# A 32-expert DiT block on one core: one more area for the weight stream, a new order of the last two experts, and the rare branch moved behind the stores

## The chip, the cores and the metric

The kernel runs on one core of one Trainium2 chip. The metric is device microseconds of one execution, the median of three runs. Weights, activations and sums are all float32, apart from a few small masks.

## The reference, cut to what matters

One block of a diffusion transformer for 256 tokens of 1024 features: modulated norm, two attentions (global and windowed), a gated merge, then a mixture of 32 experts of which each token uses four, and a last norm.

```
h2 = modulate(rms_norm(x, norm2_g), sh2, sc2)
top_logit, top_idx = top_k(h2 @ w_router + b_router, 4)
for e in range(32):
    u = h2 @ w_e1[e] + b_e1[e]                       # 1024 -> 2048
    act = glu * sigmoid(1.702 * glu) * (lin + 1)     # even and odd columns of u, clipped at 7
    out = out + combine[:, e] * (act @ w_e2[e] + b_e2[e])
x = rms_norm(x + g2 * out, final_g)
```

An expert's matrices are 8.39 MB (`w_e1`) and 4.19 MB (`w_e2`), 403 MB in all.

## The kernel before, in words

**The stream.** All large weights go through one list, `pieces`, in a fixed order. `pump` (line 96) issues them on the queue of SyncE (SP) as long as there is room: a 2 MB piece of an expert takes a whole area of 16 KB a partition, smaller pieces take half of one. `N_PAIR` (line 25) areas are allotted at the start (`areas`, line 88); after the attention `grow` (line 147) adds the buffers `xx` and `ptt` (lines 636 and 637), so that the experts have nine. `done` (line 142) gives an area back when the last matmul on it has been written into the program, and calls `pump`; on the chip SP then waits at that DMA until the readers are through. The names `ring`, `xx` and `ptt` in the profile are these areas.

**The experts.** Each expert works on up to 64 gathered tokens (`CAP`, line 19). `gather` (822) brings the tokens of a pair of experts together with matmuls, `bias1` (709) starts the sums in PSUM with the bias, `gemm1` (854) multiplies with the first matrix in eight slices `k` of 1 MB, `act` (867) does the activation on VectorE (DVE) and ScalarE (ACT), `act_turn` (880) transposes the result, and `gemm2` (890) multiplies with the second matrix. The stationary operand has 64 columns, so two matmuls share the array, one in each half of its columns. `spread` (838) makes the matrix that weighs and returns a pair's tokens, and `scatter` (912) applies it and adds to the sum `ACC`. The loop at line 974 interleaves them: scatter half of the pair before, the bias and slice 0 of expert e+1, turn e, slice 1 of e+1, `gemm2` of e, slices 2 to 7 of e+1, its activation. The order of all queues is the order of the program text (`manual_schedule`).

**The last expert** (lines 986 to 1167) has a path of its own. Its first matrix comes in eight pieces `l1`, its second in four pieces `l2`, each of 1 MB in two DMAs of 512 KB that read runs of 2 KB (lines 121 to 132). `half1` works through one half of the hidden columns, `act_half` and `turn_half` follow, `gemm2` of expert 30 stands between. Expert 30 and expert 31 are not returned as a pair: `scatter_e0` (1014) starts the sums of expert 30 in four PSUM tiles, and the last matmuls (1149) add expert 31 to them. A last norm is formed from squares of `ACC` by halves of 512 columns, and four stores of 256 KB leave at line 1167.

**The branch.** If an expert has more than 64 tokens, the block under `tc.If(cnt > CAP)` (line 1041) computes the rest for all experts. It stands between the pieces `half1(1, 1)` and `half1(1, 2)`, and with this input it is skipped, but all five engines load `cnt` (line 1040) and branch around it.

**Small DMAs.** `g2`, a gate of 1024 numbers, is written to DRAM (line 670) and read back to all partitions (751); `b2` (754) and the last norm's gain `fg` (755) come likewise. All four are issued by GpSimd (POOL).

Of the kernel before, what the change touches and what calls it, by code (L numbers as in the profile page):

```python
# [24 lines left out]
N_PAIR = 7  # L25
# [9 lines left out]
def tile_dit_block(ctx: ExitStack, tc: tile.TileContext, xcT, consts, small, rows,  # L35
                   w_m0, w_q, w_mod, w_in, w_br, w_o, w_r, w1, b1, w2, b2, out):
# [21 lines left out]
    def halves1():  # L58

        pieces.extend(("l1", q, None) for q in range(8))  # L60

    def halves2():
        pieces.extend(("l2", q, None) for q in range(4))

# [31 lines left out]
    def pump():  # L96
        while n_next[0] < len(pieces):
# [23 lines left out]
            if kind == "l2":  # L121
                h, q = divmod(idx, 2)
                for b in range(2):
                    nc.sync.dma_start(
                        out=t[:, 1024 * b:1024 * b + 1024].rearrange("p (k c) -> p k c", k=2),
                        in_=w2[NE - 1, b].rearrange("p (q k c) -> p q k c", q=2, k=2)[:, q, :, 512 * h:512 * h + 512])
            elif kind == "l1":
                h, q = divmod(idx, 4)
                for b in range(2):
                    nc.sync.dma_start(  # L130
                        out=t[:, 1024 * b:1024 * b + 1024].rearrange("p (a c) -> p a c", a=2),
                        in_=w1[NE - 1, q].rearrange("p (b a h c) -> p b a h c", b=2, a=2, h=2)[:, b, :, h, :])
            elif kind == "q":
# [536 lines left out]
    nc.gpsimd.dma_start(out=g2_dram.rearrange("o (b p) -> (o b) p", b=8), in_=g2t)  # L670
# [83 lines left out]
    nc.gpsimd.dma_start(out=be2, in_=b2)  # L754
    nc.gpsimd.dma_start(out=fg, in_=rows[0:1, 1024:2048].to_broadcast([128, 1024]))
# [98 lines left out]
    def gemm1(e, u, ks, between=None):  # L854
        p, j = divmod(e, 2)
        for k in ks:
            w = take("w1", (e, k // 2))[:, 2048 * (k % 2):2048 * (k % 2) + 2048]
# [4 lines left out]
            if k % 2:  # L862
                done("w1", (e, k // 2))
            if between and k in between:
                between[k]()
# [24 lines left out]
    def gemm2(e, aT):  # L890
# [10 lines left out]
        if e >= NE - 2:  # L901
            YY[e] = x_t[:, 0, 512 * (e % 2):512 * (e % 2) + 512]
            nc.vector.tensor_tensor(out=YY[e], in0=y, in1=g2x, op=ALU.mult)
            return
# [15 lines left out]

    def scatter_one(e, tb):

        for h in range(2):
            s = slice(512 * h, 512 * h + 512)
            sp = ps2.tile([128, 512], F32, name="sp", tag=("sp", "xg")[tb], bufs=2)
            nc.tensor.matmul(sp, TT[e][64 * h:64 * h + 64, tb, :], YY[e][64 * h:64 * h + 64, :],
                             start=True, stop=True)
            nc.vector.tensor_tensor(out=ACC[0][:, tb, s], in0=ACC[0][:, tb, s], in1=sp, op=ALU.add)

    def settle():  # L930
# [10 lines left out]
        for tb in range(2):  # L941
            for h in range(2):
# [3 lines left out]
                t = per.tile([128, 512], F32, name="bt", tag="msb")  # L946
# [12 lines left out]
    def steps(e):  # L959

        p, j = divmod(e, 2)
        if e >= NE - 2:
            return {4: lambda: spread(e, (e, e))}
        if j == 0:
            return {3: lambda: spread(p, (e, e + 1)), 5: lambda: pick(p + 1)}
# [20 lines left out]
    e0, e1 = NE - 2, NE - 1  # L986
    sums = {}

    def half1(h, q, u):
        w = take("l1", 4 * h + q).rearrange("p (b a c) -> p b a c", b=2, a=2)  # L990
        for b in range(2):
            k = 2 * q + b
            for i in range(2):
                nc.tensor.matmul(u[64 * i:64 * i + 64, h, :], XT[e1 // 2][:, k, 64:128], w[:, b, i, :],  # L994
                                 start=False, stop=(k == 7))
        done("l1", 4 * h + q)

    def act_half(h, u):
        t, c = tmp4, slice(256 * h, 256 * h + 256)
        glu, sg, lin = t[:, 0, c], t[:, 1, c], t[:, 2, c]  # L1000
        nc.vector.tensor_scalar(out=glu, in0=u[:, h, 0:256], scalar1=LIMIT, scalar2=None, op0=ALU.min)  # L1001
        nc.scalar.activation(out=sg, in_=glu, func=AF.Sigmoid, scale=ALPHA)  # L1002
        nc.vector.tensor_scalar(out=lin, in0=u[:, h, 256:512], scalar1=LIMIT, scalar2=-LIMIT, op0=ALU.min,
                                op1=ALU.max)
        nc.vector.tensor_tensor(out=glu, in0=glu, in1=sg, op=ALU.mult)
        nc.vector.scalar_tensor_tensor(out=glu, in0=lin, scalar=1.0, in1=glu, op0=ALU.add, op1=ALU.mult)

    def turn_half(h):
        tp = ps2.tile([128, 4, 128], F32, name="ta", tag="tp")
        for b in range(2):  # L1010
            nc.tensor.transpose(tp[:, b, :], tmp4[:, 0, 256 * h + 128 * b:256 * h + 128 * b + 128], ident)
        nc.scalar.copy(out=tmp4[:, 3, 256 * h:256 * h + 256].rearrange("p (b s) -> p b s", b=2), in_=tp[:, 0:2, :])  # L1012

    def scatter_e0(h):
# [5 lines left out]
    scatter(NE // 2 - 2, (0,))  # L1020
    u = bias1(e1)
    half1(0, 0, u)
    aT = act_turn(e0)
    half1(0, 1, u)
    scatter(NE // 2 - 2, (1,))
    g2x = per.tile([128, 512], F32, name="g2x", tag="msb")
    for h in range(2):
        nc.vector.tensor_copy(g2x[64 * h:64 * h + 64, :], g2[64 * h:64 * h + 64, 512 * h:512 * h + 512])
    gemm2(e0, aT)
    half1(0, 2, u)  # L1030
    half1(0, 3, u)
    act_half(0, u)
    half1(1, 0, u)
    scatter_e0(0)
    turn_half(0)
    spread(e1, (e1, e1))
    half1(1, 1, u)
# [3 lines left out]
    with tc.If(cnt > CAP):  # L1041
# [20 lines left out]
        def body(e):  # L1062
# [40 lines left out]
            for tb in range(2):  # L1103
                aT = y_t[0][:, tb, :].rearrange("p (k s) -> p k s", k=8)
                for h in range(2):
# [4 lines left out]
                    t = per.tile([128, 512], F32, name="bt", tag="msb")  # L1110
# [12 lines left out]
    nc.scalar.activation(out=junk, in_=eps, func=AF.Sqrt)  # L1123
    fin = moe.tile([128, 2, 4], F32, name="fin")
    aT = tmp4[:, 3, :].rearrange("p (b s) -> p b s", b=4)
    yl = [ps2.tile([128, 512], F32, name="yl", tag="y")]

    def half2(h, q):
        w = take("l2", 2 * h + q).rearrange("p (k c) -> p k c", k=4)
        for b in range(4):  # L1130
            k = 2 * q + 4 * (b // 2) + b % 2

            nc.tensor.matmul(yl[h][64 * (k % 2):64 * (k % 2) + 64, :], aT[:, k % 4, 64 * (k // 4):64 * (k // 4) + 64],  # L1133
                             w[:, b, :], start=(q == 0 and b < 2), stop=(q == 1 and b >= 2))

    half2(0, 0)
    turn_half(1)
    yl.append(ps2.tile([128, 512], F32, name="yl", tag="tp"))
    half2(0, 1)
    half2(1, 0)  # L1140
    for h in range(2):
        s = slice(512 * h, 512 * h + 512)
        if h:
            half2(1, 1)
        yy = x_t[:, h, 512:1024]
        nc.vector.tensor_tensor(out=yy, in0=yl[h], in1=g2[:, s], op=ALU.mult)  # L1146
        for tb in range(2):
            a = ACC[0][:, tb, s]
            nc.tensor.matmul(sums[tb, h], TT[e1][:, tb, :], yy, start=False, stop=True)  # L1149
            nc.vector.tensor_tensor(out=a, in0=a, in1=sums[tb, h], op=ALU.add)  # L1150
            nc.scalar.activation(out=y_t[0][:, tb, s], in_=a, func=AF.Square, accum_out=fin[:, tb, h:h + 1])  # L1151
            if h == 0:
                nc.vector.tensor_scalar(out=fin[:, tb, 2:3], in0=fin[:, tb, 0:1], scalar1=1.0 / 1024, scalar2=EPS,  # L1153
                                        op0=ALU.mult, op1=ALU.add)
                nc.gpsimd.tensor_tensor(out=a, in0=a, in1=fg[:, s], op=ALU.mult)
            else:
                nc.scalar.activation(out=fin[:, tb, 3:4], in_=fin[:, tb, 1:2], func=AF.Sqrt, bias=fin[:, tb, 2:3],  # L1157
                                     scale=1.0 / 1024)
    for tb in range(2):
# [99 lines left out]
```

## Time and profile before

| | |
|---|---|
| runs | 1209.86, 1210.23 and 1211.34 us; median 1210.23 us |
| the profiled execution | 1209.79 us, of which the profile's span is 1208.0 us |
| mean granted TensorE clock | 0.996 |
| busy in the span | PE 1147.9, PEld 531.5, DVE 360.0, ACT 138.8, POOL 35.1 us |
| read from HBM | 456.36 MB, on average 379 GB/s over the span |

How to read it: PE is the matmul engine, PEld its weight load, which overlaps. PE's busy time is no measure of need: matmuls are pipelined, and one that stands behind others counts as busy. The figures of the DMA engines by stretch tell more. Times in rows are microseconds from the span's start unless marked ns; an arrow in brackets names what ended an engine's idle time.

### The profile page before, as it was taken

The numbers are of one execution on the slowest core, as the hardware profiler recorded it, in microseconds if no ns is written. First come the engines' busy times: TensorE is split into PE (matmuls) and PEld (weight loads), VectorE is DVE, ScalarE is ACT, GpSimd is POOL, SyncE is SP. The second block draws the span as 40 slices with busy tenths as digits, with TensorE's granted clock in tenths as the row PEclk, the third lists the DMA queues.
The fourth block names the chain that finished last, engine by engine and source line by source line (L and its number), as shares of the span: only waits on it lengthen the run. The fifth ranks groups of instructions, "written<-read, shape, count | busy, mean of one in ns | idle before, by whom it ended". The sixth has DMA issues, their size and how long they took to land. (4 is left out here: it accounts for less than half of the span.)

```text
span 1208.0 us, 13270 instructions
## 1 busy us (share of the span) xinstructions
PE 1147.9 (95%) x5624; PEld 531.5 (44%) x5624; DVE 360.0 (30%) x765; ACT 138.8 (11%) x304; POOL 35.1 (3%) x29
## 2 busy tenths in 40 slices
PE   7999999999999999999999999999999899999986
PEld 5888666883333424343434343333333232323221
DVE  3363665332122242223222221212222222222222
ACT  2122553021000000000000000000000000000002
POOL 0231100000000000000000000000000000000000
PEclk9999999999999999999999999999999999999998
DMA  9976641978999999999999999999999999999992
GB/s 379 385 301 213 240 175 53 352 296 335 427 428 428 427 427 428 427 427 428 427 429 427 428 428 425 430 427 427 429 426 426 428 428 428 429 426 429 417 396 89
DMA packets 43279, 458.32 MB, mean 379 GB/s; under 512 B 4872, under 2 KB 5264, under 8 KB 13776
## 3 DMA queue, kind: packets, MB, share of 16 engines
q1 hardware_dynamic: 41520, 454.05, 90.3%
q10 hardware_dynamic: 1296, 2.06, 0.5%
q0 software_dynamic: 400, 1.32, 0.3%
q8 instruction: 46, 0.75, 0.2%
q14 instruction: 17, 0.14, 0.0%
HBM read 456.36 MB, written 1.05 MB: 379 GB/s over the span
## 5 line engine op out<-in xcount | busy, mean ns | idle before, releaser
L860 PE MATMUL u<-ring,t 128*64 128x512 f32 x1472 | 337.3, 599 | 19.6 <-DMA ring<-w 19.2
L860 PEld LDWEIGHTS u<-ring,t 128*64 128x64 f32 x1472 | 100.7, 137 | 214.2 <-issue 178.2
L897 PE MATMUL y<-ring,r_q 128*64 128x512 f32 x832 | 183.8, 592 | 0.0
L908 DVE TENSOR_TENSOR t<-y,r_kv 64x512 f32<-64x512 f32 x60 | 41.3, 689 | 324.8 <-PE y L897 324.4
L897 PEld LDWEIGHTS y<-ring,r_q 128*64 128x64 f32 x832 | 59.7, 137 | 118.9 <-issue 116.3
L871 DVE TENSOR_SCALAR r_q<-u 128x512 f32<-128x512 f32 x31 | 21.4, 691 | 237.0 <-PE u L860 237.0
L860 PE MATMUL u<-ptt,t 128*64 128x512 f32 x336 | 78.2, 597 | 2.5 <-DMA ptt<-w 2.2
L873 ACT ACTIVATE r_q<-r_q 128x512 f32<-128x512 f32 x31 | 19.5, 630 | 499.1 <-DVE r_q L871 499.1
L713 PE MATMUL u<-mtx,keep 128*64 128x512 f32 x256 | 62.2, 605 | 3.0 <-DVE r_q L874 3.0
L830 PEld LDWEIGHTS xg<-mtx,r_y 128*128 128x128 f32 x512 | 58.4, 192 | 12.2 <-issue 12.2
L830 PE MATMUL xg<-mtx,r_y 128*128 128x128 f32 x512 | 61.3, 278 | 0.0
L393 PE MATMUL mm<-xx,ring 128*128 128x256 f32 x256 | 59.9, 385 | 0.0
L918 PE MATMUL sp<-t,mtx 128*128 128x512 f32 x120 | 59.5, 618 | 0.0
L393 PEld LDWEIGHTS mm<-xx,ring 128*128 128x128 f32 x256 | 47.3, 190 | 12.6 <-issue 5.0
L832 DVE TENSOR_TENSOR t<-xg,modb 128x512 f32<-128x512 f32 x32 | 22.1, 691 | 88.8 <-PE xg L830 88.8
L860 PEld LDWEIGHTS u<-ptt,t 128*64 128x64 f32 x336 | 23.2, 137 | 47.6 <-issue 40.7
L860 PE MATMUL u<-xx,t 128*64 128x512 f32 x176 | 39.8, 595 | 3.8 <-DMA xx<-w 3.8
L919 DVE TENSOR_TENSOR r_t<-r_t,sp 128x512 f32<-128x512 f32 x60 | 38.4, 680 | 5.1 <-PE sp L918 5.1
L918 PEld LDWEIGHTS sp<-t,mtx 128*128 128x128 f32 x120 | 20.3, 189 | 38.9 <-issue 38.9
L897 PE MATMUL y<-xx,r_q 128*64 128x512 f32 x160 | 36.0, 592 | 0.0
L713 PEld LDWEIGHTS u<-mtx,keep 128*64 128x64 f32 x256 | 16.3, 135 | 44.5 <-issue 22.6
L887 ACT COPY r_q<-ta 128x512 f32<-128x512 f32 x31 | 18.1, 585 | 145.4 <-PE ta L884 145.4
(247 smaller groups left out, 889.9 us busy)
## 6 DMA issues: line engine op xcount, KB each, us to landing
ring<-w SPq DMA_DIRECT2D x144, 2048.0 KB, 32.2
xx<-w SPq DMA_DIRECT2D x21, 2048.0 KB, 32.4
ptt<-w SPq DMA_DIRECT2D x21, 2048.0 KB, 29.7
ring<-w_mod SPq DMA_DIRECT2D x16, 1024.0 KB, 7.2
ring<-w_in SPq DMA_DIRECT2D x10, 1024.0 KB, 9.2
ring<-w_m SPq DMA_DIRECT2D x8, 1024.0 KB, 12.6
ring<-w SPq DMA_DIRECT2D x16, 512.0 KB, 17.8
ring<-w_q SPq DMA_DIRECT2D x8, 512.0 KB, 12.3
```

The source lines that it names most:

```text
L393: nc.tensor.matmul(gp[0][:, 0:256], w[:, k, :], x[:, k, :], start=(k == 0), stop=(k == 7))
L713: nc.tensor.matmul(u[c0:c0 + 64, ch % 2, :], ident[:, 4 * e + ch:4 * e + ch + 1].to_broadcast([128, 64]), be1, start=True, stop=False)
L830: nc.tensor.matmul(xp[:, b, :], z[:, tb, 128 * k:128 * k + 128], S[:, tb, :], start=(tb == 0), stop=(tb == 1))
L832: nc.vector.tensor_tensor(out=XT[p][:, 4 * h:4 * h + 4, :], in0=xp, in1=sh2[:, 4 * h:4 * h + 4].unsqueeze(2).to_broadcast([128, 4, 128]), ...
L860: nc.tensor.matmul(u[c0:c0 + 64, ch % 2, :], XT[p][:, k, 64 * j:64 * j + 64], w[:, 512 * ch:512 * ch + 512], start=False, stop=(k == 7))
L871: nc.vector.tensor_scalar(out=glu.rearrange("p (b f) -> p b f", b=2), in0=v[:, :, 0, :], scalar1=LIMIT, scalar2=None, op0=ALU.min)
L873: nc.scalar.activation(out=sg, in_=glu, func=AF.Sigmoid, scale=ALPHA)
L887: nc.scalar.copy(out=aT, in_=tp)
L897: nc.tensor.matmul(y[64 * h:64 * h + 64, :], l, w[:, 512 * h:512 * h + 512], start=(k == 0), stop=(k == 7))
L908: nc.vector.tensor_tensor(out=YY[p][64 * j:64 * j + 64, 512 * h:512 * h + 512], in0=y[64 * h:64 * h + 64, :], in1=g2[64 * h:64 * h + 64, 5 ...
L918: nc.tensor.matmul(sp, t[:, tb, :], y[:, s], start=True, stop=True)
L919: nc.vector.tensor_tensor(out=ACC[0][:, tb, s], in0=ACC[0][:, tb, s], in1=sp, op=ALU.add)
```

## The change

- `N_PAIR` is 8 instead of 7: one more area of 16 KB a partition. Room comes from a smaller scratch for DMAs that POOL issues (`dynamic_dma_scratch_size=1024`) and from the temporary `bt`, `g2x` tile "msb", whose user `settle` now takes a part of `tmp4`.
- The four small DMAs of POOL are issued by ACT at the same places of the program.
- Expert 31's first matrix comes like the others: three pieces of 2 MB, then two pieces of 1 MB (slices 6 and 7), and `gemm1` does it whole. The second matrices of experts 30 and 31 are packed on the host as one new input `w2l`, by groups of output columns: three pieces of 2 MB with 256 columns of both experts, two pieces of 1 MB with 128 columns. The bytes are the same as before.
- `last2(c)` multiplies both experts by one group, expert 30 in one half of the array's columns and expert 31 in the other; `scatter2(c)` returns the pair's tokens for that group, adds, squares, and multiplies by `fg` on POOL. `spread` is made once for this pair, in expert 30's slice 3.
- The branch stands after the four stores; if it is taken, its end computes the last norm again and stores again.

```diff
-N_PAIR = 7
+N_PAIR = 8
...
-    halves1()
-    at = len(pieces) - 6
-    pieces[at:at] = [("w2", (NE - 2, k), w2[NE - 2, k]) for k in range(2)]
-    halves2()
+    w1s(NE - 1, range(3))
+    pieces.extend(("l1", k, w1[NE - 1, 3, :, 2048 * k:2048 * k + 2048]) for k in range(2))
+    pieces.extend(("w2", (NE, c), w2l[c]) for c in range(3))
+    pieces.extend(("l2", c, w2l[3, :, 2048 * c:2048 * c + 2048]) for c in range(2))
...
-    nc.gpsimd.dma_start(out=g2, in_=g2_dram[0:1, :].to_broadcast([128, 1024]))
+    nc.scalar.dma_start(out=g2, in_=g2_dram[0:1, :].to_broadcast([128, 1024]))
...
+    e0, e1, p = NE - 2, NE - 1, NE // 2 - 1
+    scatter(p - 1, (0,))
+    u = bias1(e1)
+    gemm1(e1, u, (0,))
+    aT0 = act_turn(e0)
+    gemm1(e1, u, range(1, 8))
+    act(e1, u)
+    scatter(p - 1, (1,))
+    nc.scalar.activation(out=junk, in_=eps, func=AF.Sqrt)
+    aT1 = act_turn(e1, tmp4[:, 1, :].rearrange("p (b s) -> p b s", b=4))
...
+    groups = [(0, 256), (256, 256), (512, 256), (768, 128), (896, 128)]
+    def last2(c):
+        n = groups[c][1]
...
+        wl[c] = ps2.tile([128, 512], F32, name="yl", tag=("y", "tp")[c % 2])
+        for k in range(8):
+            for j, aT in enumerate((aT0, aT1)):
+                nc.tensor.matmul(wl[c][64 * j:64 * j + 64, 0:n], aT[:, k % 4, 64 * (k // 4):64 * (k // 4) + 64],
+                                 w[:, j, k, :], start=(k == 0), stop=(k == 7))
...
+        nc.vector.tensor_tensor(out=y_t[0][:, 1, s], in0=wl[c][:, 0:n], in1=g2[:, s], op=ALU.mult)
+    def scatter2(c):
...
         for tb in range(2):
+            a = ACC[0][:, tb, s]
...
+            nc.tensor.matmul(sp[:, 0:n], TT[p][:, tb, :], y_t[0][:, 1, s], start=True, stop=True)
+            nc.vector.tensor_tensor(out=a, in0=a, in1=sp[:, 0:n], op=ALU.add)
+            nc.scalar.activation(out=x_t[:, tb, s], in_=a, func=AF.Square, accum_out=fin[:, tb, c:c + 1])
+            if c < 4:
+                nc.gpsimd.tensor_tensor(out=res[:, tb, s], in0=a, in1=fg[:, s], op=ALU.mult)
+            if c == 3:
+                nc.vector.reduce_sum(fin[:, tb, 5:6], fin[:, tb, 0:4], axis=AX.X)
+                nc.vector.tensor_scalar(out=fin[:, tb, 5:6], in0=fin[:, tb, 5:6], scalar1=1.0 / 1024, scalar2=EPS,
+                                        op0=ALU.mult, op1=ALU.add)
+            elif c == 4:
+                nc.scalar.activation(out=fin[:, tb, 6:7], in_=fin[:, tb, 4:5], func=AF.Sqrt, bias=fin[:, tb, 5:6],
+                                     scale=1.0 / 1024)
+    for c in range(5):
+        last2(c)
+        if c:
+            scatter2(c - 1)
+    scatter2(4)
+    for tb in range(2):
+        r = fin[:, tb, 6:7]
+        nc.vector.reciprocal(r, r)
+        nc.scalar.activation(out=res[:, tb, 0:512], in_=res[:, tb, 0:512], func=AF.Copy, scale=r)
...
+        for h in range(2):
+            nc.sync.dma_start(out=out[128 * tb:128 * tb + 128, 512 * h:512 * h + 512],
+                              in_=res[:, tb, 512 * h:512 * h + 512])
     cnt = nc.values_load(cint[0:1, 0:1], min_val=0, max_val=256)
...
-    half1(1, 2, u)
-    scatter_e0(1)
-    half1(1, 3, u)
-    act_half(1, u)
```

## Rows read from the trace of the kernel before

**Rows 1.** Windows, before the experts: us, busy of each engine, clock, DMA share, GB/s

```profile
200.00:205.00 5.00, 5.00 (x32) 3.87 (x29) 1.32 (x4) 0.24 (x1) 0.00 (x0) 1.00 0.00 0
...
275.00:280.00 5.00, 5.00 (x26) 1.61 (x24) 2.68 (x16) 0.00 (x0) 0.00 (x0) 1.00 0.30 59
```

**Rows 2.** Timeline of SP's queue, the first expert pieces: start, us issuing

```profile
205.93 0.33 SPq L136 DMA_DIRECT2D xx<-w  x1
...
222.22 42.36 SPq L136 DMA_DIRECT2D ring<-w  x7
278.02 0.33 SPq L136 DMA_DIRECT2D xx<-w  x1
```

**Rows 3.** Windows, early and late experts

```profile
500.00:600.00 100.00, 100.00 (x474) 37.83 (x472) 25.34 (x49) 5.02 (x9) 0.00 (x0) 1.00 1.01 428
...
900.00:1000.00 100.00, 91.94 (x436) 34.35 (x434) 20.60 (x38) 4.39 (x8) 0.00 (x0) 1.00 1.01 428
```

**Rows 4.** Timeline of PE, from expert 30's last slices to the last scatter

```profile
1143.34 3.65 PE L860 MATMUL u<-ring,t 128*64 128x512 f32 x16 [0.77 <-DMA ring<-w]
1146.92 1.99 PE L918 MATMUL sp<-t,mtx 128*128 128x512 f32 x4
1148.83 1.94 PE L713 MATMUL u<-mtx,keep 128*64 128x512 f32 x8
1150.60 1.89 PE L994 MATMUL u<-ring,t 128*64 128x512 f32 x8
1152.42 0.66 PE L884 MATMUL ta<-keep,r_q 128*128 128x128 f32 x4
...
1179.90 3.10 PE L994 MATMUL u<-xx,t 128*64 128x512 f32 x8 [4.70 <-PEq L1041]
1182.93 2.47 PE L1017 MATMUL sp<-t,mtx 64*128 64x512 f32 x4
...
1198.82 1.98 PE L1149 MATMUL sp<-t,mtx 128*128 128x512 f32 x4 [1.25 <-DVE t L1146]
```

**Rows 5.** Timeline of ACT: a DMA's issue, and the copies after the router

```profile
212.08 0.47 ACTq L649 DMA_DIRECT2D mtx<-w_r  x1
...
269.55 2.05 ACT L770 COPY r_t<-tx 128x512 f32<-128x512 f32 x4 [1.10 <-PE tx L769]
```

**Rows 6.** Windows at the tail: stream of 512 KB DMAs; after the branch

```profile
1160.00:1162.00 2.00, 2.00 (x13) 0.58 (x9) 0.00 (x0) 0.00 (x0) 0.00 (x0) 1.00 1.05 387
...
1182.00:1184.00 2.00, 2.00 (x6) 0.55 (x3) 0.00 (x0) 0.00 (x0) 0.00 (x0) 0.51 0.52 197
```

**Rows 7.** Timeline of DVE and ACT, an expert's activation and turn

```profile
1147.04 0.69 DVE L871 TENSOR_SCALAR r_q<-u 128x512 f32<-128x512 f32 x1 [11.20 <-PE u L860]
...
1149.21 0.69 DVE L877 SCALAR_TENSOR_TENSOR r_q<-r_q 128x512 f32<-128x512 f32 x1
...
1153.17 0.58 ACT L887 COPY r_q<-ta 128x512 f32<-128x512 f32 x1 [4.72 <-PE ta L884]
```

**Rows 8.** Timeline of PE, attention: pairs of narrow matmuls, different weights in each half

```profile
188.15 0.66 PE L567 MATMUL y<-keep,st 128*64 128x128 f32 x8 [0.41 <-DVE r_y L577]
188.63 1.90 PE L572 MATMUL y<-ptt,r_kv 128*64 128x256 f32 x16
190.46 1.99 PE L393 MATMUL mm<-xx,ring 128*128 128x256 f32 x8
```

**Rows 9.** Line 1041, branches by engine: ns min/median/max, first and last start

```profile
L1041 PEldq COMPARE_BRANCH  x1: 6172/6172/6172, 1173.6 to 1173.6; - x1
L1041 ACTq COMPARE_BRANCH  x1: 45/45/45, 1173.9 to 1173.9; - x1
L1041 SPq COMPARE_BRANCH  x1: 50/50/50, 1176.7 to 1176.7; - x1
```

**Rows 10.** Timeline of SP, the four stores

```profile
1202.76 1.91 SPq L1167 DMA_DIRECT2D out<-r_t  x4
```

**Rows 11.** Groups by line: weight load of 64 columns, mean 137 ns

```profile
L860 PEld LDWEIGHTS u<-ring,t 128*64 128x64 f32 x1472 | 100.7, 137 | 214.2 <-issue 178.2 <-DMA ring<-w 34.2
```

More of the change, by code (lines that the diff above doesn't have):

```diff
@@ L35, in tile_dit_block @@
 def tile_dit_block(ctx: ExitStack, tc: tile.TileContext, xcT, consts, small, rows,
-                   w_m0, w_q, w_mod, w_in, w_br, w_o, w_r, w1, b1, w2, b2, out):
+                   w_m0, w_q, w_mod, w_in, w_br, w_o, w_r, w1, b1, w2, b2, w2l, out):
     nc = tc.nc
@@ L56, in w2s @@
         pieces.extend(("w2", (e, k), w2[e, k]) for k in range(2))
[L58 to L63, printed above, removed]
     for j in range(10):
@@ L120, in pump @@
             held[kind, idx] = t
[L121 to L133, printed above, removed]
+            if kind == "q":
                 nc.sync.dma_start(out=t[:, 0:1024], in_=src)
@@ L669, in tile_dit_block @@
     nc.vector.tensor_copy(g2t, gp2[0:8, 0:128])
-    nc.gpsimd.dma_start(out=g2_dram.rearrange("o (b p) -> (o b) p", b=8), in_=g2t)
+    nc.scalar.dma_start(out=g2_dram.rearrange("o (b p) -> (o b) p", b=8), in_=g2t)
     g1h = moe.tile([128, 8], F32, name="g1h")
@@ L750, in tile_dit_block @@
     tmp4 = r_q.rearrange("p (a c) -> p a c", a=4)
-    nc.gpsimd.dma_start(out=g2, in_=g2_dram[0:1, :].to_broadcast([128, 1024]))
+    nc.scalar.dma_start(out=g2, in_=g2_dram[0:1, :].to_broadcast([128, 1024]))
     be2 = mtx[:, 0:2, :].rearrange("p a b -> p (a b)")
-    nc.gpsimd.dma_start(out=be2, in_=b2)
-    nc.gpsimd.dma_start(out=fg, in_=rows[0:1, 1024:2048].to_broadcast([128, 1024]))
+    nc.scalar.dma_start(out=be2, in_=b2)
+    nc.scalar.dma_start(out=fg, in_=rows[0:1, 1024:2048].to_broadcast([128, 1024]))
     nc.scalar.activation(out=junk, in_=eps, func=AF.Exp)
@@ L856, in gemm1 @@
         for k in ks:
-            w = take("w1", (e, k // 2))[:, 2048 * (k % 2):2048 * (k % 2) + 2048]
+            if e == NE - 1 and k > 5:
+                w = take("l1", k - 6)
+            else:
+                w = take("w1", (e, k // 2))[:, 2048 * (k % 2):2048 * (k % 2) + 2048]
             for ch in (0, 2, 1, 3):
@@ L861, in gemm1 @@
                                  w[:, 512 * ch:512 * ch + 512], start=False, stop=(k == 7))
-            if k % 2:
+            if e == NE - 1 and k > 5:
+                done("l1", k - 6)
+            elif k % 2:
                 done("w1", (e, k // 2))
@@ L900, in gemm2 @@
                 done("w2", (e, k // 4))
[L901 to L904, printed above, removed]
         if j == 0:
@@ L919, in scatter @@
                 nc.vector.tensor_tensor(out=ACC[0][:, tb, s], in0=ACC[0][:, tb, s], in1=sp, op=ALU.add)
[L921 to L928, printed above, removed]
     def settle():
@@ L961, in steps @@
         p, j = divmod(e, 2)
-        if e >= NE - 2:
-            return {4: lambda: spread(e, (e, e))}
+        if e == NE - 1:
+            return {}
         if j == 0:
-            return {3: lambda: spread(p, (e, e + 1)), 5: lambda: pick(p + 1)}
+            s = {3: lambda: spread(p, (e, e + 1))}
+            if e < NE - 2:
+                s[5] = lambda: pick(p + 1)
+            return s
         if e == 1:
@@ L984, in tile_dit_block @@
         act(e + 1, u)
[L986 to L1014, printed above, removed]
-        for tb in range(2):
-            sums[tb, h] = ps2.tile([128, 512], F32, name="sp", tag=("sp", "xg")[h], bufs=2)
-            nc.tensor.matmul(sums[tb, h], TT[e0][64 * h:64 * h + 64, tb, :], YY[e0][64 * h:64 * h + 64, :],
-                             start=True, stop=False)
@@ L1020, in tile_dit_block @@
[L1020 to L1037, printed above, removed]
+    e0, e1, p = NE - 2, NE - 1, NE // 2 - 1
@@ new lines, in tile_dit_block @@
+    scatter(p - 1, (0,))
[7 more added lines that the diff above has]
+    aT1 = act_turn(e1, tmp4[:, 1, :].rearrange("p (b s) -> p b s", b=4))
+    fin = moe.tile([128, 2, 8], F32, name="fin")
+    res = areas[spare[0][0]].rearrange("p (a c) -> p a c", a=4)[:, 0:2, :]
+    spare.pop(0)
+    groups = [(0, 256), (256, 256), (512, 256), (768, 128), (896, 128)]
@@ new lines, in tile_dit_block @@
+    wl = {}
+    def last2(c):
+        n = groups[c][1]
+        w = (take("w2", (NE, c)) if c < 3 else take("l2", c - 3)).rearrange("p (e k c) -> p e k c", e=2, k=8)
+        wl[c] = ps2.tile([128, 512], F32, name="yl", tag=("y", "tp")[c % 2])
[3 more added lines that the diff above has]
+                                 w[:, j, k, :], start=(k == 0), stop=(k == 7))
+        o = groups[c][0]
+        s = slice(o, o + n)
+        nc.vector.tensor_tensor(out=y_t[0][:, 1, s], in0=wl[c][:, 0:n], in1=g2[:, s], op=ALU.mult)
@@ new lines, in scatter2 @@
+    def scatter2(c):
+        o, n = groups[c]
+        s = slice(o, o + n)
+        for tb in range(2):
+            a = ACC[0][:, tb, s]
+            sp = ps2.tile([128, 512], F32, name="sp", tag=("sp", "xg")[tb], bufs=2)
+            nc.tensor.matmul(sp[:, 0:n], TT[p][:, tb, :], y_t[0][:, 1, s], start=True, stop=True)
[10 more added lines that the diff above has]
+                                     scale=1.0 / 1024)
@@ new lines, in tile_dit_block @@
+    for c in range(5):
[7 more added lines that the diff above has]
+        nc.scalar.activation(out=res[:, tb, 0:512], in_=res[:, tb, 0:512], func=AF.Copy, scale=r)
+        nc.vector.tensor_scalar(out=res[:, tb, 512:896], in0=res[:, tb, 512:896], scalar1=r, scalar2=None,
+                                op0=ALU.mult)
+        nc.vector.scalar_tensor_tensor(out=res[:, tb, 896:1024], in0=ACC[0][:, tb, 896:1024], scalar=r,
+                                       in1=fg[:, 896:1024], op0=ALU.mult, op1=ALU.mult)
+        for h in range(2):
+            nc.sync.dma_start(out=out[128 * tb:128 * tb + 128, 512 * h:512 * h + 512],
+                              in_=res[:, tb, 512 * h:512 * h + 512])
@@ L1109, in body @@
                         nc.tensor.matmul(y, aT[:, k, :], vs[k // 2][:, k % 2, s], start=(k == 0), stop=(k == 7))
-                    t = per.tile([128, 512], F32, name="bt", tag="msb")
+                    t = slots[10][:, 0:512]
                     nc.vector.tensor_tensor(out=t, in0=y, in1=g2[:, s], op=ALU.mult)
@@ L1116, in tile_dit_block @@
             body(e)
-    half1(1, 2, u)
-    scatter_e0(1)
-    half1(1, 3, u)
-    act_half(1, u)
[L1123 to L1146, printed above, removed]
-        for tb in range(2):
[L1148 to L1158, printed above, removed]
@@ L1159, in tile_dit_block @@
-    for tb in range(2):
-        res = ACC[0][:, tb, :]
-        nc.vector.reciprocal(fin[:, tb, 3:4], fin[:, tb, 3:4])
-        nc.vector.scalar_tensor_tensor(out=res[:, 512:1024], in0=res[:, 512:1024], scalar=fin[:, tb, 3:4],
-                                       in1=fg[:, 512:1024], op0=ALU.mult, op1=ALU.mult)
-        nc.scalar.activation(out=res[:, 0:512], in_=res[:, 0:512], func=AF.Copy, scale=fin[:, tb, 3:4])
-        for h in (1, 0):
-            s = slice(512 * h, 512 * h + 512)
-            nc.sync.dma_start(out=out[128 * tb:128 * tb + 128, s], in_=res[:, s])
+        for tb in range(2):
+            a, r = ACC[0][:, tb, :], fin[:, tb, 6:7]
+            nc.vector.tensor_tensor(out=x_t[:, tb, :], in0=a, in1=a, op=ALU.mult)
+            nc.vector.reduce_sum(fin[:, tb, 5:6], x_t[:, tb, :], axis=AX.X)
+            nc.scalar.activation(out=r, in_=fin[:, tb, 5:6], func=AF.Sqrt, bias=eps, scale=1.0 / 1024)
+            nc.vector.reciprocal(r, r)
+            nc.vector.scalar_tensor_tensor(out=res[:, tb, :], in0=a, scalar=r, in1=fg, op0=ALU.mult, op1=ALU.mult)
+            nc.sync.dma_start(out=out[128 * tb:128 * tb + 128, :], in_=res[:, tb, :])
@@ L1239, in _pack @@
         "b2": be2,
+        "w2l": con(np.concatenate([
+            f("w_e2")[0][30:].reshape(2, 8, 128, 4, 256)[:, :, :, 0:3].transpose(3, 2, 0, 1, 4).reshape(3, 128, 4096),
+            f("w_e2")[0][30:, :, 768:].reshape(2, 8, 128, 2, 128).transpose(2, 3, 0, 1, 4).reshape(1, 128, 4096)])),
     }
 _ORDER = ["xcT", "consts", "small", "rows", "w_m0", "w_q", "w_mod", "w_in", "w_br", "w_o", "w_r",
-          "w1", "b1", "w2", "b2"]
+          "w1", "b1", "w2", "b2", "w2l"]
 def kernel(**inputs):
@@ L1251 @@
     arrays = _pack(inputs)
-    nc = bacc.Bacc("TRN2", target_bir_lowering=False, num_devices=1)
+    nc = bacc.Bacc("TRN2", target_bir_lowering=False, num_devices=1, dynamic_dma_scratch_size=1024)
     args = [nc.dram_tensor(n, arrays[n].shape, F32, kind="ExternalInput").ap() for n in _ORDER]
```

2 lines of the change are left out of this document (1 added, 1 removed).

## The prediction

> **What bounds the kernel now.** I read the windows first, then SP's queue, then the timeline of the tail. Before the experts the DMA engines stand idle: 0.00 busy from 200 to 205 us, 0.30 from 275 to 280 [rows 1]. SP's queue says why: the first piece of expert 0 waits for `xx` until 205.93, seven pieces follow from 222.22 as the merge frees areas, and the next goes out only at 278.02, when expert 0 has read its first piece [rows 2]. Data wait for room there. Later it is the reverse. From 500 to 600 us PE is busy all the time while the stream runs at 428 GB/s, and from 900 to 1000 PE is busy 91.94 us at the same rate [rows 3]: PE is faster than the stream, eats up its lead, and then waits for each landing. So the end of the stream is fixed by how far it has got when it begins to run without pause (about 280 us), and a lead of one more area there is kept to the end. A piece is 2.097 MB, at 428 GB/s 4.90 us.
>
> At 1143.34 PE starts the last two slices of expert 30, released by their landing [rows 4]. I call this L. From L the tail is PE's: 55.48 us pass until its last scatter at 1198.82 [rows 4], and the span ends 9.2 us later.
>
> **The change part by part.** *The area.* The list is unchanged up to expert 31, and nine areas become ten. I followed `spare` through the program for both sizes: with seven ring areas none has both halves free before `grow`, with eight three do; from the piece that waited for 278.02 on, each piece takes the place in time of the one before it. The gaps of [rows 1] are filled by one piece, so L moves from 1143.34 to 1138.4: **-4.9**. Bounds: 0 if the lead is lost again, -4.9 if kept; I take the second, because the stream has no pause after 280 in [rows 3].
>
> *ACT's DMAs.* The write of `g2` waits on DVE's copy of it, with nothing behind it on ACT until the squares of the output product. The other three are issued just before the copies that free PSUM for `gather`, at 0.47 us each 1.4 us [rows 5]; behind them stand a table load and those four copies, which waited 1.10 us for PE [rows 5], and PE needs the first only after the transposes. Cost 0, without that cover at most 1.4 us. `g2` is first read when expert 0 has passed both matrices, later than the 278.02 of [rows 2] at which its first piece was read. POOL's queue loses them and nothing waits for it.
>
> *Stream of the tail.* The 512 KB DMAs move 387 GB/s [rows 6]; the new pieces have runs of 8 and 16 KB, like those that move 428. Sixteen MB after L (8.39 for expert 31's first matrix, 8.39 for `w2l`) then take 39.2 us: the groups of `w2l` land at 1162.9, 1167.8, 1172.7, 1175.1 and 1177.6. At 387 the third group would land at 1176.3 and hold PE up by 3.0 us; that is the bound above.
>
> *PE's walk from L = 1138.4*, start to start in [rows 4]: two slices 3.58, half a scatter 1.91, bias 1.77, slice 0 1.82, transposes 0.66, seven slices at 1.79 12.53: 1160.7. The activation takes 0.12 + 2.86 us (1147.04 to 1149.90, [rows 7]) and hides the other half scatter (1.91) and ACT's Sqrt table load; then transposes and copy, 1152.42 to 1153.75, 1.33 [rows 4, 7]: `last2(0)` starts at 1165.0. A group of 256 columns is 32 matmul records in 16 pairs. In the attention 16 records of that shape take 1.83 us and 8 of 128 columns 0.48 [rows 8], so a group costs 3.66 and a narrow one 1.92: 3 x 3.66 + 2 x 1.92 = 14.8. A scatter of 256 columns is half of 1.91, 0.95, a narrow one 0.48: four before the last, 3.33. The last scatter starts at 1165.0 + 14.8 + 3.33 = 1183.2. No group has to wait for its landing: they start at 1165.0, 1168.7, 1173.3, 1177.9 and 1180.8. The narrowest margin is 0.6 us.
>
> Seen as a difference from L, 55.48 - 44.8 = **-10.7**. Three terms make it. The wait of 4.70 us at the branch [rows 4] goes, because PE's branch took 6.17 us [rows 9]. Behind it the granted clock was 0.51, the lower of the two levels 1.2 and 2.4 GHz [rows 6], after PE had been idle those 4.70 us; the next eight records took 3.03 us instead of 1.82 and the scatter 2.47 instead of 1.99: 1.7. Expert 30's own scatter, two times 1.9, goes since the pair is returned together. Smaller waits balance.
>
> *The end.* Before, 3.94 us lie between the last scatter and the first store [rows 4, 10]. After, DVE has a chain in its way: the fourth group's add, ACT's square with its sum, and DVE's reduce and scale, for both token blocks in turn, because the reduce of block 0 stands ahead of block 1's add. 512 columns cost DVE 0.69 and ACT 0.58 [rows 7]; these have 128, so each step lies between a quarter and the whole of that. I estimate 0.29 for an add, 0.44 for a square with its sum, 0.36 for reduce and scale: with 0.54 for the matmuls, 2.7 us from the fourth scatter at 1182.7 to the fifth add. Then add, square and root 1.05, block 1's square and root on ACT 0.9, the copy of 512 columns 0.7: first store at 1188.1, 4.9 us after the last scatter: **+1.0**. Bounds: 0 and +2, by the same quarter and whole.
>
> *The branch at the end.* SP branches after the last store is issued; its branch took 0.05, ACT's 0.045 us [rows 9]. The stores need longer to land: the span ended 3.3 us after the last issue (1204.67, [rows 10]). PE passes its last matmul near 1183.7 and with 6.17 is through by 1190, when the last store has just been issued (1188.1 + 1.91). Cost 0; without that cover up to 6.2 (below).
>
> Sum: -4.9 - 10.7 + 1.0 = -14.6. The profiled execution took 1209.79 us, 1.79 over its span, and is 0.44 below the median of 1210.23. 1210.23 - 14.6 = **1195.6 us**.
>
> **The rivals.** *A: the branch returns at the end.* If the taken branch costs SP what it cost PE, 6.2 us stand behind the last issue. If the 3.3 us of landing and closing run beside them, that adds 2.9, in series 6.2; the middle is +4.6, 1200.2 us. For it: PE's 6.17 us at a stream-loaded moment. Against: 0.05 us on both engines in [rows 9], whose bodies under the branch are short. The Trainium skill (Runtime: NRT & Kernel Launch, Instruction fetch mechanics) says that a taken branch whose target is outside the prefetched instructions waits for a DMA fetch; by that rule each engine with a long body pays it, wherever the branch stands, and the time would be this rival's 1200.2 if SP were one; the trace agrees for PE alone.
>
> *B: the area isn't used.* If the gaps at 200 to 280 us stay, or PE or SP loses the lead later, the term of 4.9 falls away: 1200.5 us. For it: idle DMA alone doesn't prove that room is what is missing. Against: [rows 2].
>
> *C: slower.* `last2` loads two different weight sets, one into each half of the array's columns, whereas in `gemm1` both halves hold the same. If the two halves run one after the other, and loads aren't hidden, a pair costs 2 x (0.137 + 0.224) = 0.72 us for 256 columns and 2 x (0.137 + 0.112) = 0.50 for 128 (load from [rows 11]; streams half and a quarter of 0.448, the pair in [rows 4], 3.58 over 8). Then 48 x 0.72 + 32 x 0.50 = 50.6 instead of 14.8: +35.8, 1231 us. It decides from 0.40 us a pair on the average: 0.185 as forecast, and (14.6 + 2.4) / 80 = 0.21 more. Against: the rows of the attention are pairs with different weights, at 0.23 us [rows 8].
>
> **How the numbers follow.** The forecast has 0.73, with a range of its own of 1192 to 1198: the bounds of the end (1.0 either way), ACT's 1.4, and some 2 us that I allow for the walk, whose every start hangs on the one before. A has 0.12, B 0.08, C 0.03; what is left, 0.04, lies between forecast and no change. The range of 8 in 10 takes in A and B and a late landing: 1191.5 to 1201.5. Two runs of this kernel can be told apart from about 0.2%, 2.4 us: faster 0.95, within that 0.02, slower 0.03.
>
> **What would show it.** Right: DMA idle between 180 and 280 us one piece shorter and three expert pieces issued before 206; L at 1138.4; no idle of PE near 5 us and no half clock in the tail; `last2` groups of 3.7 and 1.9 us; the branch on PE ending before the last store has landed. Wrong: L within 1 us of 1143; groups over 5 us; PE waiting for `w2l`; a branch of 5 us or more on SP or ACT; a first store later than 1190.

## The result, and the profile after

The changed kernel takes 1195.74 us (median of 4 runs, 1195.13 to 1196.35), the kernel before beside it 1210.13 (4 runs): a ratio of 0.9879, 95% interval 0.9862 to 0.9896. The forecast was 1195.6. The profiled execution took 1195.13 us with a span of 1193.4, against 1209.79 and 1208.0 before, 14.6 us of span less. Timed again at the end of the study the same kernel took 1196.63 us, so differences of about 1 us between two runs of this study are not evidence by themselves.

Before the experts, the windows of the changed kernel (us, busy time of each engine with its instructions, clock, DMA share, GB/s) answer to [rows 1, 3]:

```profile
200.00:205.00 5.00, 5.00 (x32) 3.86 (x29) 1.38 (x4) 0.30 (x1) 0.00 (x0) 1.00 0.65 272
275.00:280.00 5.00, 5.00 (x26) 1.64 (x24) 2.36 (x13) 0.00 (x0) 0.00 (x0) 1.00 0.36 74
...
900.00:1000.00 100.00, 93.89 (x434) 35.16 (x434) 23.93 (x42) 4.65 (x8) 0.00 (x0) 0.98 1.01 428
```

and the timeline of SP's queue, against [rows 2] (start, us from the first to the last issue of the row):

```profile
183.90 23.14 SPq L118 DMA_DIRECT2D ring<-w  x3
207.14 0.37 SPq L118 DMA_DIRECT2D xx<-w  x1
211.78 0.33 SPq L118 DMA_DIRECT2D ptt<-w  x1
222.27 63.14 SPq L118 DMA_DIRECT2D ring<-w  x8
```

Three expert pieces go out at 183.90, 196.50 and 206.71, before `xx`. From 200 to 205 us the DMA engines are now busy at 0.65. From 277.70 us on, each piece goes out when the one before it in the list went out in the kernel before (278.02 there).

The tail, timeline of PE of the changed kernel, against [rows 4]:

```profile
1138.16 3.65 PE L845 MATMUL u<-xx,t 128*64 128x512 f32 x16 [1.24 <-DMA xx<-w]
1141.74 1.98 PE L901 MATMUL sp<-t,mtx 128*128 128x512 f32 x4
...
1149.60 10.47 PE L845 MATMUL u<-ring,t 128*64 128x512 f32 x48
1160.00 1.98 PE L901 MATMUL sp<-t,mtx 128*128 128x512 f32 x4
1163.13 0.63 PE L871 MATMUL ta<-keep,r_q 128*128 128x128 f32 x4 [1.14 <-ACT junk L971]
1163.69 7.87 PE L985 MATMUL yl<-ring,r_q 128*64 128x256 f32 x64
1171.48 1.13 PE L997 MATMUL sp<-t,mtx 128*128 128x256 f32 x4
1172.58 3.67 PE L985 MATMUL yl<-ring,r_q 128*64 128x256 f32 x32
1176.18 1.13 PE L997 MATMUL sp<-t,mtx 128*128 128x256 f32 x4
1177.25 1.97 PE L985 MATMUL yl<-ring,r_q 128*64 128x128 f32 x32
1179.14 1.13 PE L997 MATMUL sp<-t,mtx 128*128 128x256 f32 x4
1180.20 1.97 PE L985 MATMUL yl<-ring,r_q 128*64 128x128 f32 x32
1182.10 1.18 PE L997 MATMUL sp<-t,mtx 128*128 128x128 f32 x8
```

L is at 1138.16 instead of 1143.34. Behind it PE's rows show one wait, 1.14 us for ACT; a second one, 0.55 us for ACT's copy of expert 31's turn, lies inside the row at 1163.69, whose third matmul starts at 1164.43. Neither the wait of 4.70 us nor the rows at half clock are there, and no group waits for `w2l`. A group of 256 columns takes 3.60 us start to start (1172.58 to 1176.18), a narrow one 1.89. The last row holds the fourth and the fifth scatter.

The first store goes out at 1186.95. From the last scatters the chain of work that ended last leads to it (start, us, what), block 0 and block 1 in turn as expected:

```profile
1182.63 0.30 DVE r_t L998
...
1182.95 0.41 ACT t L999 x2
...
1183.38 0.17 DVE fin L1003
...
1183.58 0.15 DVE fin L1004
...
1184.39 0.17 DVE fin L1003
...
1186.22 0.57 ACT ring L1018
...
1186.83 0.72 ACT ring L1018
```

The first store needs the copy of block 0, at 1186.22; the last row is the copy of block 1, behind the first store.

The branch, by engine (ns min/median/max, first and last start), against [rows 9]:

```profile
L1029 PEldq COMPARE_BRANCH  x1: 3602/3602/3602, 1183.2 to 1183.2; - x1
...
L1029 DVEq COMPARE_BRANCH  x1: 76/76/76, 1187.6 to 1187.6; - x1
L1029 ACTq COMPARE_BRANCH  x1: 45/45/45, 1187.7 to 1187.7; - x1
L1029 SPq COMPARE_BRANCH  x1: 50/50/50, 1190.3 to 1190.3; - x1
```

And the stores, from issue to landing (line 1024 of the changed kernel):

```profile
L1024 SPq DMA_DIRECT2D out<-ring x4: 343/444/840, 1187.0 to 1188.8; - x4
...
DMA to landing us min/median/max: 3.0/3.1/3.4
```

The span splits at two marks, L and the first store:

| | before | forecast | after |
|---|---|---|---|
| start to L | 1143.34 | -4.9 | 1138.16 (-5.2) |
| L to first store | 59.42 | -9.7 (-10.7 + 1.0) | 48.79 (-10.6) |
| first store to end of span | 5.2 | 0 | 6.4 (+1.2) |
| sum | 1208.0 | -14.6 | 1193.4 (-14.6) |

The sum is right to a tenth because two errors of about 1 us cancel. The last line is the one that the prediction had at nothing.

### The profile page after: what moved, and what is told of

Its sections match the earlier page's. It is cut to its first block, busy times and chain, and to the rows that moved or that the text cites. A ratio compares the mean times of both kernels' runs of the same rounds, so it can differ in the third digit from the quotient of the medians.

```text
span 1193.4 us, 13447 instructions
## 1 busy us (share of the span) xinstructions
PE 1142.9 (96%) x5722; PEld 539.0 (45%) x5722; DVE 359.4 (30%) x767; ACT 139.5 (12%) x313; POOL 35.7 (3%) x31
## 4 chain that ended last, share of the span: by engine, by line
PE 57%; DMA 36%; DVE 4%; ACT 2%; issue 1%; ACTq 0%; SPq 0%; DVEq 0%
DMA ring<-w 26%; PE u L845 20%; DMA xx<-w 10%; PE y L884 9%; PE mm L375 3%; PE xg L812 3%; PE u L695 3%; PE qa L276 2%; PE o L705 2%; PE sp L901 2%; PE br L579 2%; ACT xx L517 1%; PE yl L985 1%; PE kp L365 1%; PE vp L449 1%; DVE st L507 1%
## 5 line engine op out<-in xcount | busy, mean ns | idle before, releaser
L845 PE MATMUL u<-ring,t 128*64 128x512 f32 x1632 | 373.8, 598 | 16.1 <-DMA ring<-w 15.7
L845 PEld LDWEIGHTS u<-ring,t 128*64 128x64 f32 x1632 | 112.6, 137 | 233.3 <-issue 201.2
L884 PE MATMUL y<-ring,r_q 128*64 128x512 f32 x768 | 168.9, 592 | 0.0
L884 PEld LDWEIGHTS y<-ring,r_q 128*64 128x64 f32 x768 | 55.2, 137 | 109.6 <-issue 107.9
L845 PE MATMUL u<-xx,t 128*64 128x512 f32 x208 | 48.7, 610 | 3.7 <-DMA xx<-w 3.6
L845 PE MATMUL u<-ptt,t 128*64 128x512 f32 x208 | 48.8, 598 | 0.9 <-DMA ptt<-w 0.9
L276 PE MATMUL qa<-xx,ring 128*128 128x256 f32 x128 | 30.7, 388 | 0.0
L845 PEld LDWEIGHTS u<-xx,t 128*64 128x64 f32 x208 | 14.7, 139 | 35.3 <-issue 28.1
```

The costliest lines, as they stand in the source:

```text
L276: nc.tensor.matmul(qa[c // 4][:, c % 4, :], w[:, 128 * c:128 * c + 128], x[:, j, :], start=(j == 0 and c % 2 == 0), stop=(j == 7), skip_gr ...
L884: nc.tensor.matmul(y[64 * h:64 * h + 64, :], l, w[:, 512 * h:512 * h + 512], start=(k == 0), stop=(k == 7))
```

## The experiments

**The area alone.** Both ways round: the area taken out of the changed kernel, and put into the kernel before.

```diff
-N_PAIR = 8
+N_PAIR = 7
...
-        slots = [half(s) for s in spare]
+        slots = [half(s) for s in spare] + [half(s) for v in place.values() for s in v]
```

(the slots are the skipped branch's.) 

> The changed kernel with seven areas again instead of eight (nine instead of ten for the experts). Theory: the area is worth its one piece and nothing else, so expert 30's last slices start at 1143.1 instead of 1138.16 and all behind them is 4.9 us later: 1200.6 us. Rival (the tail is PE's own and takes up a late stream): less than 2 us, under 1197.7 us.

```diff
-N_PAIR = 7
+N_PAIR = 8
...
-    nc.gpsimd.dma_start(out=be2, in_=b2)
+    nc.scalar.dma_start(out=be2, in_=b2)
```

(in the kernel before; all four small DMAs move to ACT, POOL's scratch is made smaller, and three small tiles are laid into others to make room). 

> The kernel before with the area alone (and what makes room for it: the small DMAs on ACT, less scratch, no extra tile for the bias). Theory: the old tail too hangs on the landing of expert 30's last slices, so it gains the same 4.9 us: 1205.2 us, with the 4.7 us wait at the branch unchanged. Rival (in the old tail something else sets the end, and the lead turns into a longer wait): 1209 to 1211 us.

The second is as expected: 1205.68 us (ten runs, 1204.64 to 1212.18; the kernel before beside it 1210.73), ratio 0.9967 (0.9953 to 0.9981), L at 1138.26, the wait at the branch still 4.69 us. The first came out above what either theory had, at 1204.13 us, 8.4 more than the changed kernel: L stood at 1146.52, 3.2 us later than in the kernel before, which has as many areas. Its first expert piece (`xx`) was issued at 209.31 against 205.93 [rows 2], so the delay was all there before the stream. Part of it lay in the attention, where the narrow pairs of [rows 8] took 3.58 us instead of 1.90 at half clock (timeline of PE, first experiment):

```profile
147.39 0.67 PE L549 MATMUL y<-keep,st 128*64 128x128 f32 x8 [2.08 <-DVE r_y L559]
147.87 3.58 PE L554 MATMUL y<-ptt,r_kv 128*64 128x256 f32 x16
```

So the same build was run once more, on another chip. 

> The same build as the first experiment: the changed kernel with seven areas. There L came 8.4 us later than in the changed kernel, 3.4 us more than the area's 4.9, and those 3.4 us were all there by the first expert pieces (209.31 against 205.93): 0.9 us by 37 us of the span, some 0.7 more by 145 us, and 1.7 from two batches of narrow value matmuls at half clock at 147.9 us. Theory, that these are chances of one execution (piece landings and the clock in attention) and no work of the area: L near 1143.1 and 1200.6 us. Rival, that seven areas and ScalarE's queue together delay the first part each time: L at 1146.5 again, and 1204.1 us.

It took 1202.55 us (1201.54 to 1204.96), its first expert piece left at 206.66 and L was at 1144.10; the changed kernel beside it took 1196.63. From the first expert piece to L it is 937.4 us in the kernel before, 937.2 and 937.4 in these two: the stream repeats to 0.2 us. What differs is when it begins, and that moved by 2.7 us between two profiles of one build. The area is worth 5.1 us by the second experiment, in the medians as in L; by the last pair it is 5.4 in the spans (1199.8 and 1194.4) and 5.9 in the medians.

**The branch alone.** Left out of each kernel (both then lack the overflow branch, which is skipped with these inputs).

```diff
-    cnt = nc.values_load(cint[0:1, 0:1], min_val=0, max_val=256)
-    with tc.If(cnt > CAP):
...
```

> The changed kernel without the branch and the block under it; with this input the block is skipped, so the output is the same. Theory as forecast (the branch behind the stores is covered by their landing): no change, 1195.7 us, the span still ending 4.1 us after the last store's issue. Rival (it isn't fully covered: the engines' code comes in beside the stores, whose first one landed 2.98 us after its issue against 2.09 before): 1 us or a little more back, 1194.5 us, landing again near 2.1 us.

> The kernel before without the branch and its block, output the same. Theory: PE's wait of 4.7 us and the half clock behind it (1.7 us) go, 6.4 us: 1203.7 us. Rival (the wait covered something that comes late anyway, such as the last pieces of the stream, which land at 1186.6): 2 us or less, 1208 us or more.

The kernel before without it takes 1203.40 us, ratio 0.9935 (0.9918 to 0.9952), a span 6.4 us shorter: PE goes from slice to slice without the 4.70 us and without the half clock, as its timeline in that kernel shows:

```profile
1173.59 1.94 PE L994 MATMUL u<-ring,t 128*64 128x512 f32 x8
1175.36 1.89 PE L994 MATMUL u<-xx,t 128*64 128x512 f32 x8
1177.17 1.98 PE L1017 MATMUL sp<-t,mtx 64*128 64x512 f32 x4
```

The two terms that the prediction summed for it, 4.70 and 1.7, make 6.4. Counted from L, which came 0.3 us later here (1143.65), it is 6.7 us to the last scatter (48.80 instead of 55.48). The changed kernel without it takes 1194.82 us, a span of 1192.5, 0.9 shorter, though its first store leaves 0.09 us later (1187.04). That is the rival's forecast and not the theory's. The stores land sooner (line 1024, that kernel):

```profile
L1024 SPq DMA_DIRECT2D out<-ring x4: 347/384/395, 1187.0 to 1188.5; - x4
...
DMA to landing us min/median/max: 2.1/2.8/3.2
```

The branch at the end is thus not free: beside it SP's longest issue was 840 ns instead of 395, and no store landed in under 3.0 us.

**The branch in the middle of expert 31's first matrix.** The block moved between slices 5 and 6 (it doesn't form the norm there), with the second half of expert 30's scatter ahead of it. 

> The changed kernel with the branch in PE's dense work, between slices 5 and 6 of expert 31, as it stood between two pieces of that expert before (its block no longer forms the norm at its end). Theory: the old price comes back, a wait of 4 to 5 us on PE plus the half clock behind it, 5.5 to 6.5 us in all, less up to 1 us that the stores win at the end: about 1200.7 us. Rival (the wait was due to the old place, where the stream of 2 KB runs held up the fetch): 2 us or less, 1197.7 us.

1201.39 us, ratio 0.9915 (0.9892 to 0.9939), as the theory had it. PE's timeline of that kernel shows the parts:

```profile
1160.72 3.65 PE L845 MATMUL u<-ring,t 128*64 128x512 f32 x16 [2.41 <-PEq L972]
1167.42 1.09 PE L871 MATMUL ta<-keep,r_q 128*128 128x128 f32 x4 [3.05 <-ACT junk L1051]
1168.43 9.92 PE L1065 MATMUL yl<-ring,r_q 128*64 128x256 f32 x64
```

The branch took PE 6.09 us, of which 2.41 show as idle; the wait for ACT is 3.05 instead of 1.14, because the scatter that hid it had gone ahead; and then the first two groups ran partly at half clock (granted 0.50 until 1173), 9.92 us instead of 7.87.

**The halves in series.** Rival C, made to happen as far as the order of issue can:

```diff
-        for k in range(8):
-            for j, aT in enumerate((aT0, aT1)):
+        for j, aT in enumerate((aT0, aT1)):
+            for k in range(8):
```

> The changed kernel with last2's loops exchanged: all eight matmuls of expert 30 for a group, then all eight of expert 31, so that neighbours share a half of the array's columns. Same sums. Theory: two neighbours in different halves run side by side only because they stand next to each other; apart, a pair of 256 columns costs 0.45 us instead of 0.22 and the five groups 28 us instead of 14: about 1209 us. Rival (the array finds the pairs itself, or loads and order do not matter): 1195.7 us.

1204.95 us, ratio 0.9946 (0.9927 to 0.9966): 9.2 us slower than the changed kernel, less than expected. PE's timeline of that kernel:

```profile
1175.87 6.31 PE L985 MATMUL yl<-ring,r_q 128*64 128x256 f32 x32
1182.11 1.13 PE L997 MATMUL sp<-t,mtx 128*128 128x256 f32 x4
1183.17 3.33 PE L985 MATMUL yl<-ring,r_q 128*64 128x128 f32 x32
```

A pair costs 6.24 / 16 = 0.39 us for 256 columns and 3.26 / 16 = 0.20 for 128, where side by side it is 0.225 and 0.118. So the two halves do run side by side in the change, with different weights, and even in series a pair stays well below the 0.72 and 0.50 us of rival C. It is less even than the two streams alone that C counted (2 x 0.224 and 2 x 0.112), so no time of the weight loads shows. By the groups alone the five would cost 10.7 us more; from L to the first store it is 9.1 (57.86 instead of 48.79). Part of the difference is that the first eight matmuls no longer wait 0.55 us for expert 31's turn; the rest was not traced.

**The scatter twice.** Each scatter matmul of the five groups issued twice with the same result. 

> The changed kernel with each of the ten matmuls of the last scatter made twice; the second overwrites the first, output the same. It prices the separate scatter of expert 30 that the change saved. Theory: eight of 256 and 128 columns more stand on PE's path ahead of the fifth group, 0.45 us for a matmul of 256 columns, in all 3.3 us and half a us at the fifth: 1199.3 us. Rival (PE has slack there, because the groups wait for their landing or for DVE): under 1 us, 1196.5 us.

1198.56 us, ratio 0.9890 (0.9866 to 0.9914), 2.8 above the changed kernel. A doubled scatter takes 1.99 us instead of 1.13, 0.86 more; three of them lie on PE's path in full, the last shows 0.2 at the first store. The tail is PE's, as the prediction read it.

**The chain at the end.** The two reduces of the sums of squares moved behind the fifth group's adds.

```diff
-            if c == 3:
-                nc.vector.reduce_sum(fin[:, tb, 5:6], fin[:, tb, 0:4], axis=AX.X)
...
     scatter2(4)
+    for tb in range(2):
+        nc.vector.reduce_sum(fin[:, tb, 5:6], fin[:, tb, 0:4], axis=AX.X)
...
```

> The changed kernel with the sums over the first four groups of squares formed behind the fifth group's adds instead of ahead of them. Same output. Theory: DVE waits for ACT twice for 0.47 us ahead of the fifth adds and spends 0.6 us on the sums; out of the way they leave the first store about 1 us earlier: 1194.7 us. Rival (the roots then wait for the sums, or the stores' landing and the branch set the end anyway): 1195.7 us.

1194.87 us, ratio 0.9861 (0.9839 to 0.9882), too near the changed kernel to tell. The profile is clearer: the fourth scatter starts at 1182.71 and the first store leaves at 1186.05, 3.34 us later instead of 4.85. The chain is 1.5 us shorter. But the span is 1193.3: L came 0.6 us later in this execution, and the stores landed after 3.1 to 4.3 us, beside the branch.

**The branch under the stream.** If a branch costs only what waits for it, expert 26 should hide it, where PE waits for landings anyway.

```diff
         gemm2(e, aT)
+        if e == 26:
+            cnt = nc.values_load(cint[0:1, 0:1], min_val=0, max_val=256)
+            with tc.If(cnt > CAP):
...
         gemm1(e + 1, u, range(2, 8), steps(e + 1))
```

> The changed kernel with the branch moved from behind the stores to expert 26, where TensorE waits for the stream anyway (the skipped block would use areas that hold weights, and does not form the norm). Theory, that a branch costs the end only what TensorE or the stores wait for it: TensorE's branch of some 6.1 us comes out of its later waits for pieces, pieces are issued late but still land back to back, L stays at 1138.2, and the end is that of the kernel without the branch: 1194.8 us. Rival, that a late area release delays the stream, or TensorE does not catch up: up to 6.1 us more, 1200.9 us.

> Both small things together: the branch at expert 26 and the two reduces of the sums of squares behind the fifth group's adds. Theory: first store 3.3 us behind the last scatter's start instead of 4.85 (as in the eighth experiment), stores land undisturbed, so 0.9 and 1.5 us off the changed kernel: 1193.3 us. Rival, that the earlier stores gain nothing since the last store waits for other work: 1194.8 us.

> The changed kernel itself once more beside these, to hold them against: 1195.7 us. If it comes at 1194.8 or lower, the small gains of the last two are not told from chance.

Both theories fell: 1227.14 us, ratio 1.0142 (1.0125 to 1.0159), and 1225.54 with the shorter chain, against 1196.63 for the changed kernel beside them. PE's own branch took 5.85 us there. What costs most of the 31 us is SP. Timeline of SP, and of PE, in the first of the two:

```profile
1030.51 15.00 SPq L118 DMA_DIRECT2D ring<-w  x4
1084.51 0.34 SPq L118 DMA_DIRECT2D xx<-w  x1
1090.44 0.33 SPq L118 DMA_DIRECT2D ptt<-w  x1
```

```profile
1032.14 7.04 PE L884 MATMUL y<-ring,r_q 128*64 128x512 f32 x32
1074.56 3.68 PE L845 MATMUL u<-xx,t 128*64 128x512 f32 x8 [35.38 <-SPq L962]
1079.44 3.62 PE L845 MATMUL u<-xx,t 128*64 128x512 f32 x8 [1.19 <-SPq L962]
```

and the branch's line, then the waits of SP's queue (us in total, times, longest):

```profile
L962 SPq EVENT_SEMAPHORE  x8: 17/17/17, 1054.9 to 1084.3; - x8
```

```profile
SPq L962 <- SPq L962: 37.8, 7, 8.5
```

Where the ways join again, SP passes eight semaphore instructions, the first at 1054.9 and the last at 1084.3. They end with the landings of the pieces under way (1054.90 for one issued at 1015.83, 1084.22 for the last, issued at 1045.18). Until then SP issues nothing: 39 us of lead are gone, the queue runs empty, and PE, which is released by SP's instructions here, gets a piece that landed at 1040.24 only at 1074.56. The stores land after 2.1 to 2.7 us in both kernels, and the shorter chain brings the first store from 4.86 to 3.33 us behind the fourth scatter here too; in the medians it is worth 1.6 us, little more than two runs of one kernel differ.

No version of these beats the changed kernel by more than runs of it differ.

## Why the prediction was right, and where it was off

**The area**: right, -5.2 for -4.9 in the profile, and -5.1 alone in the kernel before (L 1138.26); rival B falls with it. The list takes one more piece into the gaps of [rows 1] and keeps that lead. The windows show the lead being used up later: from 700 to 800 us PE is busy 99.69 us, where it had 95.45 before.

**ACT's DMAs**: no cost seen. In the second experiment they are there with the area, and L moves by its whole piece; and with seven areas the way from the first expert piece to L is 937 us with them as without them.

**The stream of the tail**: right. `w2l` lands at 1162.66, 1167.55, 1172.44 and 1174.90 for 1162.9, 1167.8, 1172.7 and 1175.1, and the DMA engines fall idle at 1177.0, where the fifth was forecast for 1177.6; the DMA engines move 426 GB/s from 1160 to 1162, where [rows 6] had 387. PE waits for none of them.

**PE's walk**: right in each part, a little long in the sum. To the fourth scatter the forecast had 44.3 us from L (1138.4 to 1182.7), the trace 43.94. Groups were 3.60 and 1.89 for 3.66 and 1.92, the scatters of 256 columns 1.06 to 1.10 for 0.95, slices 1 to 7 together 12.16 for 12.53. Of its three terms, the branch's wait and the half clock are shown by the fourth experiment (6.4 to 6.7 us together). The third, expert 30's own scatter, has no experiment that puts it back: its rows are gone from the trace, and the seventh experiment shows that more scatter here lies on PE's path, at 0.86 us for 256 columns.

**The end**: the mechanism was right, the reduce of block 0 ahead of block 1's add, and the eighth experiment takes 1.5 us from it. From the fourth scatter to the first store it was 4.85 us for the 5.4 forecast (1182.7 to 1188.1): the squares took 0.41 and reduce and scale 0.35, near the estimates of 0.44 and 0.36. Most of the difference is block 1's square and root on ACT, 0.53 us (1185.69 to 1186.22) for 0.9.

**The branch at the end**: this step failed: "Cost 0". It was argued from SP's own 0.05 us, and that held; rival A's mechanism, a long branch on SP or ACT, didn't occur. But the argument asked which engine waits, and not what the stores meet on their way. From the first store to the end of the span it is 6.4 us instead of 5.2; leaving the branch out gave 0.9 us of span back. Over all profiles the two cases stand apart. In the seven in which no branch stands behind the stores (the kernel before among them) the quickest store takes 2.0 to 2.1 us from issue to landing, and the span ends 5.2 to 5.8 us after the first store; in the seven that have one there it is 2.4 to 3.1 and 6.4 to 7.3.

What the stores meet shows in the rows of the DMA queues. Between the first store's issue and the last landing the changed kernel (1187 to 1191.5 us) moves three packets of instructions, two of 8 KB and one of 16 KB, the latter for about 0.9 us (packets, MB, share):

```profile
q8 instruction: 1, 0.02, 1.2%
q14 instruction: 2, 0.02, 1.0%
```

The one without a branch (1187 to 1191.3 us) moves one:

```profile
q14 instruction: 1, 0.01, 0.4%
```

The other profiles go with it: three or four such packets beside the stores in each of the seven that have the branch there, none in the remaining six. The middle store lands after 2.3 to 2.4 us where there is none, 2.8 with the one packet, 2.8 to 3.8 with three or four. So code was moved beside the stores wherever they landed late; that a packet held up a given store, and why SP's issues are longer too, was not shown.

PE stood at its branch in every place tried: 6.17, 6.09 and 5.85 us beside the stream, 3.60 behind it. The rule of the Trainium skill that rival A named (Runtime: NRT & Kernel Launch, Instruction fetch mechanics) fits that; ACT, DVE, POOL and SP passed theirs in 0.045 to 0.076 us, and no run here shows whether that is because their bodies are shorter.

**Rival C**: refuted by the groups' times; the sixth experiment shows that the order of issue makes the halves overlap, and that C's price was about twice the real one.

## What to carry to other kernels

A branch that is never entered had three prices here: the wait of PE (6.4 us with the half clock behind it), the queue that sees its transfers land before it goes on (31 us in the middle of a stream), and a little of what runs beside it at the end (about 1 us, with code moved beside the stores). Look for the place where no transfer is still to be issued and no engine has work left; that is what the change does. And a lead that was gained once, where data waited for room, lasted here through some 900 us of a stream that ran without pause.

## What had not been expected

- SP's eight semaphore instructions behind a branch are in the kernel before as well, at 1177.2 to 1186.6, and cost nothing there, because SP had no more pieces to issue. The same rows under the stream cost 31 us.
- PE's branch took 3.60 us with the stream over (3.34 to 3.88 in the seven profiles that have it there), against 5.85 to 6.19 beside it.
- Two profiles of one build put the start of the stream 2.7 us apart (209.31 and 206.66), 1.7 of it from one stretch of attention at half clock; the 937 us behind it repeat to 0.2. Such shifts can explain differences of a few us between kernels whose tails are the same.
- Adjacent matmuls that fill the same half of the columns took 0.195 us each for 256 columns; alternating between the halves, 0.112.
